# Two-layer hybrid block on one core: the second layer's first products in another order, and queries and keys copied out of PSUM ahead of their norms

## The chip, the cores and the metric

One core of one Trainium2 chip runs the whole program. The metric is the device time of one execution, in microseconds (us). Names used: PE is TensorE, DVE is VectorE, ACT is ScalarE, POOL is GpSimd, SP is the engine that issues the DMAs.

## What is computed

Two trunk layers over 512 latent tokens and 256 context tokens, 1024 features wide, in fp32:

```python
for l in range(2):
    h  = modulate(rms_norm(x,  g_mix[l]), sh1,  sc1)      # latents
    hc = modulate(rms_norm(xc, g_mix[l]), csh1, csc1)     # context
    aq, ak, av, bu, bv, cin, dq, dk, dv = split_cols(h @ w_in[l])
    # the last layer takes only the keys and values of A and D from the context
    out_a = window_attention(rope(rms_norm(aq)), rope(rms_norm(ak)), av, ...)
    out_b = spatial_gating(bu, bv, ...)
    out_c = multiscale_pool(cin, ...)
    out_d = neighbourhood_attention(rms_norm(dq), rms_norm(dk), dv, ...)
    x = x + g1 * (concat(out_a, out_b, out_c, out_d) @ w_out[l])
    x = x + g2 * swiglu(modulate(rms_norm(x, g_ffn[l]), sh2, sc2))
    # and the same for xc, in the first layer only
```

## The kernel before

**Numbers.** Every large product is made of three matmuls (`mm3`, lines 65 to 67): each operand is split into a high and a low fp32r half, and high x high, high x low and low x high are summed in PSUM. Weights come by DMA into `raw` (3 buffers) and are split by ACT (line 82) and DVE or POOL (line 83) into `w` (6 buffers) or `mraw`.

**Layout.** The stream is kept feature-major: eight tiles `x` of 128 features x 768 tokens, latents in columns 0 to 511, context in 512 to 767. The norm over features is a matmul with ones over the sum of squares (`norm_scale`, line 290), a reciprocal root by ten small DVE steps (`rsqrt`, lines 100 to 109), and a matmul that spreads the root over the partitions (`norm_spread`, line 299), which ACT copies to a `row` tile, called `r` (line 301).

**First products.** Three column groups of the input projection, C (two halves) and the values of D (two halves), don't wait for the norm: `scaled` multiplies `x` by its gain only, and the root is multiplied in when the result is taken out of PSUM. Their PSUM banks are `pj` x2 (first half of C), `sc` x2 (second half of C), `po` and `pt` (first half of D's values), and `tq` and `md` (second half of D's values), so all eight banks are full when they end. `c_take` empties the `pj` and `sc` banks (line 784), `d_values` the others (lines 586 to 596).

**Normed input.** The other groups take `h`, eight tiles made by `normed` (lines 304 to 316): for latents and then for context of each of the eight k, gain and root (DVE line 313, or ACT line 310 and POOL line 311 for the k in a list), shift (ACT line 314) and low half (DVE line 315).

**Queries and keys.** `tok_proj` makes two token tiles of 256 columns in one bank (`pj` or `sc`, 48 matmuls). `post_qk` then squares them from PSUM on ACT (line 479), sums (DVE line 481), takes the root (`rsqrt`), multiplies by it from PSUM (DVE line 484), then gain, rotary, transposes into `tq` (PE line 510) and splits into the tiles that attention reads (lines 525, 526 and 531 to 533). The tiles of `post` have 4 buffers. In the second layer the order in the program is `d_ctx` (keys of D from the context), `d_proj(0)`, the attention of D's first pair, `d_proj(1)`, and so on to A and B.

**Order.** Each engine works through its own queue in order. The queues are written at build time by a scheduler that takes program order as priority and places instructions by its own estimate of when they can start; `issue_after(ins)` puts an instruction behind another one on its engine.

Of the kernel before, what the change touches and what calls it, by code (L numbers as in the profile page):

```python
# [39 lines left out]
def hybrid_block(ctx: ExitStack, tc, t, out):  # L40
# [9 lines left out]
    def tile(tag, shape, dtype=F32):  # L50
        return sb.tile(shape, dtype, tag=tag, name=tag, bufs=BUFS[tag])
# [217 lines left out]
    class Squares:  # L269
# [5 lines left out]
        def add(self, x, eng=V):  # L275
# [6 lines left out]
            S.activation(sq[:, :n], x[:, :n], AF.Square)  # L282
            eng.tensor_add(self.acc[:, :n], self.acc[:, :n], sq[:, :n])

    def norm_scale(sq, segs):

        n = segs[-1][1] // 128
        ps = psum("tq")
        for i in range(n):
            T.matmul(ps[:, i:i + 1], sq.acc[:, 128 * i:128 * i + 128], ones[:, 0:1], start=True, stop=True)  # L290
        return rsqrt(ps[:, :n], n, 1.0 / D, EPS)

    def norm_spread(r, segs, tags):

        out = tile("row", [128, NT])
        for (s0, s1, v), tag in zip(segs, tags):
            bc = psum(tag)
            for i in range(s0 // 128, s1 // 128):
                T.matmul(bc[:, 128 * i - s0:128 * i - s0 + 128], r[:, i:i + 1].to_broadcast([128, 128]), ident,
                         start=True, stop=True)  # L300
            S.activation(out[:, s0:s1], bc[:, :s1 - s0], AF.Copy)
        return out

    def normed(x, r, gain, sh, eng):

        h = tile("h", [128, 2, NT], F32R)
        for s0, s1, v in segs_all:
            u, hi, lo = x[:, s0:s1], h[:, 0, s0:s1], h[:, 1, s0:s1]
            if eng is G:
                S.activation(u, u, AF.Copy, scale=gain[:, v:v + 1])  # L310
                G.tensor_mul(u, u, r[:, s0:s1])
            else:
                V.scalar_tensor_tensor(u, u, gain[:, v:v + 1], r[:, s0:s1], op0=OP.mult, op1=OP.mult)
            S.activation(hi, u, AF.Identity, bias=sh[:, v:v + 1])
            V.scalar_tensor_tensor(lo, u, sh[:, v:v + 1], hi.bitcast(F32), op0=OP.add, op1=OP.subtract)
        return h

    def per_feature(m, u, k):
        return m[:, u, k // 4, k % 4]
# [65 lines left out]
    for l in range(DEPTH):  # L385
# [13 lines left out]
        if l == 0:  # L399
            xs, hu, ready = [None] * KT, [None] * KT, set()  # L400
            sq = Squares(segs_all)
            ws = [[], [], []]
            for what, k in START.split():
                k = int(k)
                if what == "w":
                    for w, (name, g) in zip(ws, first):
                        w += wsplit(t[name][0, g][:, 512 * k:512 * k + 512])
                    continue
                if what == "s":
                    mod_slab(k, mods[0], bg)  # L410
                else:
                    xs[k] = load_x(t["xt"][:, k])
                    sq.add(xs[k], G if k in (1, 3, 4, 5, 6, 7) else V)
                if k in ready:
                    hu[k] = scaled(xs[k], a[:, 0, k], shift(k), segs_all)
                ready.add(k)
                if what + str(k) == "s4":
                    rr = norm_scale(sq, segs_all)
                if what + str(k) == "s5":
                    r = norm_spread(rr, segs_all, ("md", "md"))  # L420
            first = ws
            mods.append(new_mod(1))
        else:
            r = norm_spread(norm_scale(sq, segs_all), segs_all, ("tq", "tq"))
            first = [feat_units(*x) for x in first]
        fcuts = [cuts_lat if last else cuts_all] * 2 + [cuts_all]
        pss = [[psum(x) for x in y] for y in (("pj", "pj"), ("sc", "sc"), ("po", "pt"))]
        for k in range(KT):
            for w, ct, ps in zip(first, fcuts, pss):
                scaled_proj(w, hu[k], ct, ps, k)  # L430
        pss.append([psum(x) for x in ("tq", "md")])
        w = feat_units("win_dv", 1, "mraw")
        for k in range(KT):
            scaled_proj(w, hu[k], cuts_all, pss[3], k)
        h = []
        for k in range(KT):
            with behind([3, -1, 7, 7, 7, 7, 7, 7][k] if l == 0 else -1):
                h.append(normed(xs[k], r, a[:, 0, k], shift(k), G if k in [[0, 1, 3, 6], [0, 3, 6]][l] else V))


        if l == 0:
# [31 lines left out]
        def post_qk(ps, b, nq, nk, gain, ng, rope, Q, K, window, c0=0):  # L473

            nh = nq + nk
            p3 = ps.rearrange("p (i x) -> p i x", i=2)[:, :, c0:c0 + 64 * nh].rearrange("p i (h d) -> p i h d", d=64)
            flat = "p i h d -> p (i h) d"
            s2 = tile("post", [128, 2, nh, 64])
            S.activation(s2, p3, AF.Square)
            ss = small.tile([128, 8], F32, tag="ss", name="ss")  # L480
            V.tensor_reduce(ss[:, :2 * nh], s2.rearrange(flat), axis=AX.X, op=OP.add)
            r = rsqrt(ss[:, :2 * nh], 2 * nh, 1.0 / 64, EPS).rearrange("p (i h) -> p i h", i=2)
            n_ = tile("post", [128, 2, nh, 64])
            V.tensor_tensor(n_, p3, r.unsqueeze(3).to_broadcast([128, 2, nh, 64]), op=OP.mult)
            if ng:
                V.tensor_tensor(n_[:, :, 0:ng], n_[:, :, 0:ng],
                                gain.unsqueeze(1).unsqueeze(1).to_broadcast([128, 2, ng, 64]), op=OP.mult)
            if rope:
                rot = tile("post", [128, 2, nh, 64])
                for i in range(2):  # L490
                    nv = n_[:, i].rearrange("p h (x f c) -> p h x f c", x=2, f=2)
                    rv = rot[:, i].rearrange("p h (x f c) -> p h x f c", x=2, f=2)
                    sv = sinT[:, b + i].rearrange("p (x f c) -> p x f c", x=2, f=2)
                    for f in range(2):
                        V.tensor_tensor(rv[:, :, :, f], nv[:, :, :, 1 - f],
                                        sv[:, :, f].unsqueeze(1).to_broadcast([128, nh, 2, 16]), op=OP.mult)
                V.tensor_tensor(n_, n_, cosT[:, b:b + 2].unsqueeze(2).to_broadcast([128, 2, nh, 64]), op=OP.mult)
                V.tensor_add(n_, n_, rot)
            t0 = 128 * b

            w = window and b < 4
            pt = psum("tq")
            for j in range(nh // 2):
                for i in range(2):
                    dst = pt[:, 256 * j:256 * j + 256]
                    if w and 2 * j < nq:
                        dst = dst.rearrange("p (w i r c) -> p i r w c", w=4, i=2, r=2)[:, i]
                    else:
                        dst = dst[:, 128 * i:128 * i + 128]
                    T.transpose(dst, n_[:, i, 2 * j:2 * j + 2], ident)  # L510
            halves = [slice(64 * e, 64 * e + 64) for e in range(2)]
            for j in range(nh // 2):
                src = pt[:, 256 * j:256 * j + 256]
                if 2 * j < nq:

                    for e in range(2):
                        own, other = [Q[j][halves[x], e] for x in (e, 1 - e)]
                        if w:
                            own, other = [x[:, :SEQ].rearrange("p (w y x) -> p w y x", w=4, y=2)[:, :, b // 2]
                                          for x in (own, other)]  # L520
                            y = src[halves[e]].rearrange("p (w x) -> p w x", w=4)
                        else:
                            own, other = [x[:, t0:t0 + 256] for x in (own, other)]
                            y = src[halves[e]]
                        S.activation(own, y, AF.Copy)
                        V.tensor_sub(other, y, own.bitcast(F32))
                else:

                    for e in range(2):
                        own, other = [K[0][halves[x], e, t0:t0 + 256] for x in (e, 1 - e)]  # L530
                        S.activation(own, src[halves[e]], AF.Copy)
                        S.activation(other, src[halves[e]], AF.Copy)
                        V.tensor_sub(K[1][halves[e], e, t0:t0 + 256], src[halves[e]], own.bitcast(F32))
# [312 lines left out]
                             nsink[:, p:p + 3:2], mix[p])  # L846

        if last:
            csh = [c_take(c, pss[c]) for c in range(2)]
            v0 = d_values(pss[2], "row")  # L850
            v1 = d_values(pss[3], "mraw")
            kc = d_ctx()
            q0 = d_proj(0, kc[0])
# [9 lines left out]
            a_group(1, *ga)  # L863
            b_fin(*gb)
        else:
            csh = [c_take(c, pss[c]) for c in range(2)]
            v0 = d_values(pss[2], "row")
            v1 = d_values(pss[3], "mraw")
# [227 lines left out]
```

## Time and profile before

| | us |
|---|---|
| median of three runs | 1555.96 |
| the three runs | 1555.71 to 1559.7 |
| the profiled execution | 1556.92 |
| its span, first to last instruction | 1555.1 |
| PE busy in the span | 1514.8 |
| DVE busy in the span | 957.6 |
| ACT busy in the span | 620.8 |

All times below are us from the start of the span of the profiled execution. The second layer begins at about 930; its input projection and attention last until about 1147, and the output projection and the feed-forward part follow.

### The profile page before, as it was taken

How to read it: one execution, taken by the hardware profiler on the slowest of the kernel's cores; microseconds unless marked ns; L12 is line 12 of the kernel's file. 1: busy time of each engine (PE TensorE's matmuls, PEld its weight loads, DVE VectorE, ACT ScalarE, POOL GpSimd, SP SyncE). 2: the span in 40 equal slices, each digit the busy share in tenths (PEclk: the TensorE clock that was granted, in tenths of full speed). 3: DMA queues.
4: the chain of work that ended last, by engine and by line, in shares of the span. 5: the costliest groups of instructions: out<-in, count | busy, mean ns of one | idle time of the engine just before them, and what ended most of it. 6: DMA issues, size and time to landing. Idle time of an engine off the chain costs nothing.

```text
span 1555.1 us, 26167 instructions
## 1 busy us (share of the span) xinstructions
PE 1514.8 (97%) x10098; PEld 1332.3 (86%) x10098; DVE 957.6 (62%) x2317; ACT 620.8 (40%) x1278; POOL 113.6 (7%) x107
## 2 busy tenths in 40 slices
PE   7899999999999999999999998899999999999999
PEld 4688787788888888888888887888889998998997
DVE  4689877686486624843384467789956553454553
ACT  5547655643322112221222354467754332332331
POOL 2321200100000000000000004432000000000000
PEclk9899999999999999999999999999999999999999
DMA  8343223342243313622272231211233233323223
GB/s 311 119 149 100 87 87 108 124 140 74 88 143 123 109 65 112 223 60 68 90 243 65 75 114 55 80 34 44 64 102 101 95 91 99 94 85 103 95 84 100
DMA packets 79324, 163.39 MB, mean 105 GB/s; under 512 B 12000, under 2 KB 17760, under 8 KB 79200
## 3 DMA queue, kind: packets, MB, share of 16 engines
q1 hardware_dynamic: 79200, 161.73, 32.7%
q8 instruction: 79, 1.29, 0.3%
q14 instruction: 45, 0.37, 0.1%
HBM read 157.50 MB, written 4.19 MB: 104 GB/s over the span
## 4 chain that ended last, share of the span: by engine, by line
PE 88%; DVE 6%; DMA 3%; ACT 1%; issue 1%; SPq 0%; POOL 0%; ACTq 0%; POOLq 0%
PE pj L65 9%; PE pj L66 9%; PE pj L67 9%; PE sc L65 6%; PE sc L66 6%; PE sc L67 6%; PE tq L65 3%; PE tq L66 3%; PE po L66 3%; PE po L65 3%; PE tq L67 3%; PE po L67 3%; PE po L349 3%; PE pt L66 2%; PE pt L65 2%; PE pt L67 2%
## 5 line engine op out<-in xcount | busy, mean ns | idle before, releaser
L82 ACT ACTIVATE w<-raw 128x512 fp32r<-128x512 f32 x368 | 227.8, 622 | 627.0 <-PE sc L67 157.0
L83 DVE TENSOR_TENSOR w<-raw,w 128x512 fp32r<-128x512 f32 x336 | 226.2, 676 | 241.2 <-ACT w L82 240.5
L65 PE MATMUL pj<-w,h 128*128 128x256 f32 x480 | 139.6, 291 | 13.2 <-DVE x L784 7.7
L66 PE MATMUL pj<-w,h 128*128 128x256 f32 x480 | 139.2, 290 | 0.0
L67 PE MATMUL pj<-w,h 128*128 128x256 f32 x480 | 138.8, 290 | 0.0
L66 PE MATMUL pj<-st,w 128*128 128x258 f32 (+2 forms) x384 | 120.0, 313 | 3.0 <-DVE st L254 3.0
L65 PE MATMUL pj<-st,w 128*128 128x258 f32 (+2 forms) x384 | 120.2, 314 | 1.4 <-ACT st L253 1.2
L66 PE MATMUL sc<-st,w 128*128 128x258 f32 (+2 forms) x384 | 119.3, 311 | 0.0
L67 PE MATMUL pj<-st,w 128*128 128x258 f32 (+2 forms) x384 | 119.3, 311 | 0.0
L65 PE MATMUL sc<-st,w 128*128 128x258 f32 (+2 forms) x384 | 119.2, 311 | 0.0
L67 PE MATMUL sc<-st,w 128*128 128x258 f32 (+2 forms) x384 | 118.8, 310 | 0.0
L65 PEld LDWEIGHTS pj<-w,h 128*128 128x128 f32 x480 | 93.3, 194 | 20.4 <-issue 10.4
L83 POOL TENSOR_TENSOR w<-raw,w 128x512 fp32r<-128x512 f32 x32 | 42.6, 1342 | 747.5 <-ACT w L82 723.0
L66 PEld LDWEIGHTS pj<-w,h 128*128 128x128 f32 x480 | 93.4, 195 | 1.8 <-issue 0.9
L67 PEld LDWEIGHTS pj<-w,h 128*128 128x128 f32 x480 | 93.2, 194 | 0.4 <-issue 0.3
L65 PEld LDWEIGHTS pj<-st,w 128*128 128x128 f32 x384 | 73.0, 190 | 8.4 <-ACT st L253 2.4
L66 PEld LDWEIGHTS pj<-st,w 128*128 128x128 f32 x384 | 72.7, 189 | 7.8 <-DVE st L254 3.2
L67 PEld LDWEIGHTS pj<-st,w 128*128 128x128 f32 x384 | 72.6, 189 | 5.5 <-issue 1.7
L65 PEld LDWEIGHTS sc<-st,w 128*128 128x128 f32 x384 | 72.8, 190 | 4.5
L66 PEld LDWEIGHTS sc<-st,w 128*128 128x128 f32 x384 | 72.4, 188 | 4.2
L67 PEld LDWEIGHTS sc<-st,w 128*128 128x128 f32 x384 | 72.3, 189 | 4.0
L65 PE MATMUL po<-st,w 128*128 128x512 f32 (+1 forms) x192 | 66.1, 344 | 0.0
(308 smaller groups left out, 4122.1 us busy)
## 6 DMA issues: line engine op xcount, KB each, us to landing
mraw<-in_wmod SPq DMA_DIRECT2D x80, 512.0 KB, 3.7
raw<-in_wg SPq DMA_DIRECT2D x88, 256.0 KB, 2.6
raw<-in_wu SPq DMA_DIRECT2D x88, 256.0 KB, 2.6
raw<-in_wd SPq DMA_DIRECT2D x64, 256.0 KB, 2.7
h<-in_wslab SPq DMA_DIRECT2D x16, 512.0 KB, 7.9
raw<-in_wout SPq DMA_DIRECT2D x32, 256.0 KB, 2.6
x<-in_xt SPq DMA_DIRECT2D x16, 384.0 KB, 5.7
raw<-in_wd SPq DMA_DIRECT2D x32, 192.0 KB, 2.4
```

What stands on the lines that cost most here:

```text
L65: T.matmul(ps, ah, bh, start=start, stop=False)
L66: T.matmul(ps, ah, bl, start=False, stop=False)
L67: T.matmul(ps, al, bh, start=False, stop=stop)
L82: S.activation(w[:, 0, :n], raw, AF.Copy)
L83: eng.tensor_sub(w[:, 1, :n], raw, w[:, 0, :n].bitcast(F32))
L349: T.matmul(o[64 * hh:64 * hh + 64, :128], vs[hh][lo:hi], pts[i, hh], start=i == 0, stop=i == n - 1)
```

## The change

Four edits. In the second layer the first products run group by group (all eight k of one group) in place of k by k, with the norm's matmuls placed by `issue_after`: the ones-matmuls are issued before unit 6 (of 24 units, eight k for each of three groups) and the spreading ones before unit 10. `norm_spread` spreads the context segment before the latent one, everywhere it is used, and in the second layer into two banks (`tq` and `md`) in place of one. `normed` works on one segment at a time: the context of all eight k first; the latents follow later in program order, in the second layer the first two k ahead of `c_take` and the rest behind the first `d_values`. POOL's list of k in the second layer becomes 2, 4, 6 in place of 0, 3, 6. In `post_qk`, in both layers, ACT copies the queries and keys from PSUM to a `post` tile, ahead of the squares, and DVE multiplies the copy by the root in place.

```diff
     def norm_spread(r, segs, tags):
...
-        for (s0, s1, v), tag in zip(segs, tags):
+        for (s0, s1, v), tag in reversed(list(zip(segs, tags))):
...
-    def normed(x, r, gain, sh, eng):
-
-        h = tile("h", [128, 2, NT], F32R)
-        for s0, s1, v in segs_all:
-            u, hi, lo = x[:, s0:s1], h[:, 0, s0:s1], h[:, 1, s0:s1]
+    def normed(h, x, r, gain, sh, eng, seg):
+
+        s0, s1, v = seg
+        u, hi, lo = x[:, s0:s1], h[:, 0, s0:s1], h[:, 1, s0:s1]
...
-            r = norm_spread(norm_scale(sq, segs_all), segs_all, ("tq", "tq"))
+            r = norm_spread(norm_scale(sq, segs_all), segs_all, ("tq", "md"))
...
-        for k in range(KT):
-            for w, ct, ps in zip(first, fcuts, pss):
-                scaled_proj(w, hu[k], ct, ps, k)
+        if last:
+
+            for j, (w, ct, ps) in enumerate(zip(first, fcuts, pss)):
+                for k in range(KT):
+                    with ExitStack() as st:
+                        for mark, n in (("scale", 6), ("spread", 10)):
+                            if 8 * j + k >= n:
+                                st.enter_context(tc.issue_after(marks[mark].ins))
+                        scaled_proj(w, hu[k], ct, ps, k)
+        else:
+            for k in range(KT):
+                for w, ct, ps in zip(first, fcuts, pss):
+                    scaled_proj(w, hu[k], ct, ps, k)
...
-                h.append(normed(xs[k], r, a[:, 0, k], shift(k), G if k in [[0, 1, 3, 6], [0, 3, 6]][l] else V))
+        h = [tile("h", [128, 2, NT], F32R) for _ in range(KT)]
+
+        def normalise(seg, k0=0, k1=KT):
+            for k in range(k0, k1):
+                with behind([3, -1, 7, 7, 7, 7, 7, 7][k] if l == 0 else -1):
+                    normed(h[k], xs[k], r, a[:, 0, k], shift(k), G if k in [[0, 1, 3, 6], [2, 4, 6]][l] else V, seg)
+
+        normalise(segs_all[1])
...
+            n_ = tile("post", [128, 2, nh, 64])
+            S.activation(n_, p3, AF.Copy)
             s2 = tile("post", [128, 2, nh, 64])
             S.activation(s2, p3, AF.Square)
...
-            n_ = tile("post", [128, 2, nh, 64])
-            V.tensor_tensor(n_, p3, r.unsqueeze(3).to_broadcast([128, 2, nh, 64]), op=OP.mult)
+            V.tensor_tensor(n_, n_, r.unsqueeze(3).to_broadcast([128, 2, nh, 64]), op=OP.mult)
...
         if last:
+
+            normalise(segs_all[0], 0, 2)
             csh = [c_take(c, pss[c]) for c in range(2)]
             v0 = d_values(pss[2], "row")
+            normalise(segs_all[0], 2)
             v1 = d_values(pss[3], "mraw")
...
         else:
+            normalise(segs_all[0])
             csh = [c_take(c, pss[c]) for c in range(2)]
```

## Rows read from the trace of the kernel before

**Rows 1.** Page, busy time of each engine.

```profile
PE 1514.8 (97%) x10098; PEld 1332.3 (86%) x10098; DVE 957.6 (62%) x2317; ACT 620.8 (40%) x1278; POOL 113.6 (7%) x107
```

**Rows 2.** Waits of PE, 930 to 1150: total, times, longest.

```profile
PE pj L65 <- DVE x L784: 7.2, 1, 7.2
PE pj L65 <- ACT st L532: 4.9, 1, 4.9
```

**Rows 3.** Busy time by stage: window, length, engines, granted PE clock, DMA.

```profile
60.00:340.00 280.00, 275.77 (x2077) 231.76 (x2077) 224.96 (x669) 163.11 (x382) 36.51 (x37) 0.99 0.34 111
961.50:1050.00 88.50, 73.64 (x572) 69.64 (x574) 72.55 (x223) 46.37 (x107) 34.70 (x34) 0.92 0.16 53
1050.00:1110.00 60.00, 60.00 (x514) 53.93 (x511) 56.15 (x192) 42.38 (x104) 8.76 (x7) 1.00 0.14 46
1110.00:1147.00 37.00, 37.00 (x263) 29.37 (x263) 23.84 (x71) 23.03 (x52) 0.00 (x0) 1.00 0.32 101
```

**Rows 4.** Timeline of PE, second layer's first products: start, duration.

```profile
930.12 0.28 PE L65 MATMUL pj<-st,w 128*128 128x256 f32 x1
...
936.77 1.40 PE L290 MATMUL tq<-ones,row 128*128 128x1 f32 x12
...
943.34 1.05 PE L299 MATMUL tq<-ident,ry 128*128 128x128 f32 x8
...
947.68 0.60 PE L299 MATMUL tq<-ident,ry 128*128 128x128 f32 x4
...
961.07 0.28 PE L67 MATMUL md<-st,mraw 128*128 128x258 f32 x1
```

**Rows 5.** Timeline of DVE over the same stretch.

```profile
933.27 0.95 DVE L283 TENSOR_TENSOR row<-row 128x768 f32<-128x768 f32 x1
...
938.20 0.17 DVE L100 TENSOR_SCALAR rx<-tq 128x6 f32<-128x6 f32 x1 [3.58 <-PE tq L290]
...
945.07 6.61 DVE L313 SCALAR_TENSOR_TENSOR x<-x,a,row 128x512 f32<-128x512 f32 x5 [4.88 <-ACT row L301]
...
959.10 3.44 DVE L313 SCALAR_TENSOR_TENSOR x<-x,a,row 128x256 f32<-128x256 f32 x5
...
964.86 3.24 DVE L315 SCALAR_TENSOR_TENSOR h<-x,mod,h 128x256 fp32r<-128x256 f32 x8
...
970.21 0.41 DVE L586 TENSOR_TENSOR mraw<-md,row 128x256 f32<-128x256 f32 x1
```

**Rows 6.** Timeline of ACT: the roots' copies, and a square of queries and keys.

```profile
944.43 0.60 ACT L301 ACTIVATE row<-tq 128x512 f32<-128x512 f32 x1 [2.10 <-PE tq L299]
...
951.67 0.36 ACT L301 ACTIVATE row<-tq 128x256 f32<-128x256 f32 x1
...
998.64 0.60 ACT L479 ACTIVATE post<-pj 128x512 f32<-128x512 f32 x1
```

**Rows 7.** Chain that ended last, 936 to 1060: PE after its two waits.

```profile
968.58 0.55 PE pj L65
...
971.48 0.15 PE pj L65
971.99 0.12 PE pj L66
...
1006.64 0.55 PE pj L65
...
1012.10 0.21 PE pj L65
```

**Rows 8.** Timeline of DVE ahead of the second wait.

```profile
990.99 3.42 DVE L100 TENSOR_SCALAR rx<-ss 128x8 f32<-128x8 f32 x1
...
1005.80 0.69 DVE L484 TENSOR_TENSOR post<-pj,ry 128x512 f32<-128x512 f32 x1
```

**Rows 9.** Single line: duration min/median/max in ns, first and last start.

```profile
L484 DVE TENSOR_TENSOR post<-pj,ry x21: 406/691/693, 92.0 to 1076.8; 128x512 f32<-128x512 f32 x13, 128x256 f32<-128x256 f32 x8
```

**Rows 10.** Single line: the gain after it, from SBUF; columns as before.

```profile
L486 DVE TENSOR_TENSOR post<-post,d_q_gain x10: 406/422/1382, 93.5 to 1012.2; 128x256 f32<-128x256 f32 x10
```

More of the change, by code (lines that the diff above doesn't have):

```diff
@@ L283, in add @@
             eng.tensor_add(self.acc[:, :n], self.acc[:, :n], sq[:, :n])
+    marks = {}
     def norm_scale(sq, segs):
@@ L289, in norm_scale @@
         for i in range(n):
-            T.matmul(ps[:, i:i + 1], sq.acc[:, 128 * i:128 * i + 128], ones[:, 0:1], start=True, stop=True)
+            marks["scale"] = T.matmul(ps[:, i:i + 1], sq.acc[:, 128 * i:128 * i + 128], ones[:, 0:1],
+                                      start=True, stop=True)
         return rsqrt(ps[:, :n], n, 1.0 / D, EPS)
@@ L295, in norm_spread @@
         out = tile("row", [128, NT])
-        for (s0, s1, v), tag in zip(segs, tags):
+        for (s0, s1, v), tag in reversed(list(zip(segs, tags))):
             bc = psum(tag)
             for i in range(s0 // 128, s1 // 128):
-                T.matmul(bc[:, 128 * i - s0:128 * i - s0 + 128], r[:, i:i + 1].to_broadcast([128, 128]), ident,
-                         start=True, stop=True)
+                marks["spread"] = T.matmul(bc[:, 128 * i - s0:128 * i - s0 + 128],
+                                           r[:, i:i + 1].to_broadcast([128, 128]), ident, start=True, stop=True)
             S.activation(out[:, s0:s1], bc[:, :s1 - s0], AF.Copy)
         return out
-    def normed(x, r, gain, sh, eng):
-        h = tile("h", [128, 2, NT], F32R)
-        for s0, s1, v in segs_all:
-            u, hi, lo = x[:, s0:s1], h[:, 0, s0:s1], h[:, 1, s0:s1]
[L309 to L316, printed above, removed]
+    def normed(h, x, r, gain, sh, eng, seg):
+        s0, s1, v = seg
+        u, hi, lo = x[:, s0:s1], h[:, 0, s0:s1], h[:, 1, s0:s1]
+        if eng is G:
+            S.activation(u, u, AF.Copy, scale=gain[:, v:v + 1])
+            G.tensor_mul(u, u, r[:, s0:s1])
+        else:
+            V.scalar_tensor_tensor(u, u, gain[:, v:v + 1], r[:, s0:s1], op0=OP.mult, op1=OP.mult)
+        S.activation(hi, u, AF.Identity, bias=sh[:, v:v + 1])
+        V.scalar_tensor_tensor(lo, u, sh[:, v:v + 1], hi.bitcast(F32), op0=OP.add, op1=OP.subtract)
     def per_feature(m, u, k):
@@ L427, in hybrid_block @@
         pss = [[psum(x) for x in y] for y in (("pj", "pj"), ("sc", "sc"), ("po", "pt"))]
-        for k in range(KT):
-            for w, ct, ps in zip(first, fcuts, pss):
-                scaled_proj(w, hu[k], ct, ps, k)
+        if last:
[6 more added lines that the diff above has]
+                        scaled_proj(w, hu[k], ct, ps, k)
+        else:
+            for k in range(KT):
+                for w, ct, ps in zip(first, fcuts, pss):
+                    scaled_proj(w, hu[k], ct, ps, k)
         pss.append([psum(x) for x in ("tq", "md")])
@@ L434, in hybrid_block @@
             scaled_proj(w, hu[k], cuts_all, pss[3], k)
-        h = []
-        for k in range(KT):
-            with behind([3, -1, 7, 7, 7, 7, 7, 7][k] if l == 0 else -1):
-                h.append(normed(xs[k], r, a[:, 0, k], shift(k), G if k in [[0, 1, 3, 6], [0, 3, 6]][l] else V))
+        h = [tile("h", [128, 2, NT], F32R) for _ in range(KT)]
[4 more added lines that the diff above has]
+        normalise(segs_all[1])
         if l == 0:
```

## The prediction

> **What bounds the kernel now.** I read the page's busy times first: PE works 1514.8 of the span's 1555.1 us, and DVE 957.6 [rows 1]. So PE sets the time, its work is not changed, and the change can only win what PE loses between its matmuls, or lose by adding to it. Next the waits of PE in the second layer's projection and attention: one of 7.2 us on `c_take` (line 784) and one of 4.9 us that is put down to line 532 [rows 2]. The table by stage says what that is of the whole: from 961.5 to 1050 PE is busy 73.6 of 88.5 us, so 14.9 are lost, the two waits and 2.8 us of small ones; from 1050 to 1147 nothing is lost [rows 3]. The reader is to see there also that DVE is busy 56.2 of the 60 us from 1050 on: it is a second engine close to its limit, right behind the place where the gain would be.
>
> **Why PE waits at 961.** The last first product ends at 961.35 [rows 4], and PE starts on the context's keys at 968.58 [rows 7]. Those need a `pj` bank and the context part of all eight `h`. The timeline of DVE shows a block without a gap from 945.07 to 970.62: latents' line 313, their line 315, the context's line 313 only at 959.10, its line 315 last of all at 964.86, and `c_take` behind that [rows 5]. The block starts at 945.07 because `r` is late: the squares' sum is done at 934.22 [rows 5], the ones-matmuls start at 936.77, the spreading at 943.34, and the context's spreading at 947.68 [rows 4], as it waits for the one bank that ACT is copying from. ACT's copies end at 945.03 and 952.03 [rows 6].
>
> **The head of the layer, after.** I put the new order on the clock of the old one. First products start at 930.12 [rows 4]; a matmul of 256 columns takes 0.12 [rows 7], so a unit of six takes 0.72, and the six units ahead of the ones-matmuls end at 934.4, when the sum (934.22) is there. The ones-matmuls take 1.40 [rows 4]: 935.8. The root is ten DVE steps of 0.17 [rows 5], with gaps some 2.0: 937.8. Four units cover it, to 938.7. Spreading took 1.05 + 0.60 [rows 4]; the context's third of it comes first, then its copy of 0.36 [rows 6]: context `r` at about 939.6, latent `r` (0.60 to copy) at about 941. That is 12 and 4 us earlier. DVE's block was 25.55 us long [rows 5] with nothing idle; started at 939.6 it ends at 965.1. In it the context comes first: five of 0.69 (3.44 / 5) and eight of 0.41 (3.24 / 8), 6.7 us, to 946.3; two k of latents, four operations of 1.32 (6.61 / 5), to 951.6; `c_take`, four operations of 256 columns at the 0.41 of line 586 and two tiny ones, 1.8, to 953.4. PE needs both at 961.35, 8 us later. The work that hides the block is the rest of the first products; without it (were `r` late as before) the wait would be back whole. What is late next is the latents' `h`: PE has 48 matmuls of the context, 5.8 us, to 967.1, and the block ends at 965.1. Two us of slack, so I cost it at nothing. The weights pass no queue that gets longer: the first group's two `w` buffers come free after eight units in place of half-way through all, and the steps moved issue no DMA; the constants' DMAs on SP wait for none of them.
>
> The wait costs more than 7.2. After it PE's matmuls stand 0.21 apart, half speed, until 971.48: 12 in 2.90 us where 12 x 0.12 = 1.44 would do [rows 7]. The mean granted clock from 961.5 to 1050 is 0.92 [rows 3]. So the head is worth 7.2 + 1.5 = **8.7 us**, and I take it whole; its lower bound is 0 (below).
>
> **The copy ahead of the norms.** The second wait, 4.9 us long [rows 2], ends at 1006.64 [rows 7], just when line 484 (1005.80 + 0.69) has read the bank [rows 8]: the row names line 532, the bank is what is waited for. Line 484 is late because the root ahead of it sat behind a DVE step of 3.42 us [rows 8], 0.17 elsewhere [rows 5]. With the copy the bank is free when ACT has read it twice. Here ACT squared at 998.64 in 0.60 [rows 6]; with the copy before it the bank is free at 999.9, ahead of the 1001.7 at which PE comes to it. The bank wait goes, and with it the half-speed stretch behind it, 24 matmuls in 5.46 us where 2.88 would do: 4.9 + 2.6 = 7.5 us at most. What can be late next: a tile of `post` is now held from the copy to the transposes, and there are four; and DVE has the same chain to do. Between 0 and 7.5 I take **5.0**, nearer to the upper end since the row shows the bank free in time, and less than all since DVE's 3.42 is not touched. The small waits, 2.8 us, hang on the same chains of DVE in attention: between 0 and 2.8, taken **0.8**.
>
> What it adds: 23 copies on ACT, 0.36 to 0.60 each, some 12 us over two layers. ACT is busy 42 of 60 us at its fullest here [rows 3], so they fit; each also stands ahead of its square, in the latency of its chain. In the first layer PE is busy 275.8 of 280 us from 60 on [rows 3]: the other reorderings there can win 4.2 at most, and the 12 copies of that layer can lose up to 7 if all were on the path. I take 0.
>
> DVE's multiplication changes from a PSUM source to an SBUF one. From PSUM line 484 never took over 0.69 [rows 9]. Line 486, with its operands in SBUF, takes 0.42 as a rule and 1.38 at worst [rows 10]; laid beside POOL's timeline, its long ones are those under a POOL instruction. The second layer has eleven of line 484, nine of them before 1050, where POOL is busy 34.7 of 88.5 us [rows 3]: some three would lie under POOL, so 0 to 3 x 0.96 = 2.9 us of DVE. I take **1.0** lost, as not each lands on the path. The Trainium skill (SBUF — State Buffer, "SBUF: two separate sides") has a rule that speaks against this edit: a DVE operation with two SBUF inputs and a GpSimd one that reads SBUF take one port pair by turns, and the loser waits out the whole instruction. By that rule the copy buys its bank with all 2.9 us, if DVE sets the end; the trace agrees as far as the 1.38 goes.
>
> **Sum.** 8.7 + 5.0 + 0.8 - 1.0 = 13.5 us off. The profiled execution took 1556.92, 1.8 more than its span, and would take 1543.4; the median of the runs is 0.96 below it, so 1542.5.
>
> **Rivals.**
> *All of it goes.* 8.7 + 7.5 + 2.8 = 19.0, and some of the first layer's 4.2. For it: from 1110 to 1147 DVE is busy only 23.8 of 37 us [rows 3], so it can take work earlier. Time 1535 to 1537.
> *DVE takes over.* The head is won, but DVE is busy 94% from 1050 to 1110 [rows 3], the matmuls that fill PE there run out sooner, and the second and the small waits come back on softmax or on `post`. Against it: DVE also starts 5 us earlier and no longer stands idle between 970.6 and the first squares of the context's keys. 8.7 less 1.0 to 2.9: time 1547 to 1550, or 1552 if half the head returns as well.
> *The change does not do what it says.* The queues are fixed from an estimate. If DVE's queue has `d_values` of the third group, or POOL's k, before their inputs are there, the block waits for PE at 952 and the latents' `h` is late by as much as was won. Time 1553 to 1557.
> *Slower: the copies hold ACT.* A copy that finds no free `post` tile stops ACT's whole queue, with the exponentials and the weight splits behind it, until an earlier chain's transposes are done. The only price of such a chain here is PE's wait of 4.9 [rows 2]: five of the 23 at 4.9 cost 24.5 against 13.5 won, 1567. It decides from 18.2 us on, 0.8 for each copy. Against it: three chains fit the four tiles unless rotary takes a third.
>
> **How the numbers follow.** Forecast 0.42 (its own range 1538 to 1547), all of it 0.15, DVE takes over 0.25, not as said 0.08, slower 0.10. Faster, by over 0.3% (4.7 us, about what a measurement of this kernel can tell from no change), is the first three: 0.82; same 0.08; slower 0.10. The range from 1535 to 1553 leaves out the slower case and most of the fourth.
>
> **What would show it.** The ones-matmuls at about 934.4 and spreading by 940, context first. DVE's block starting near 939.6, with line 784 ahead of most of the latents. No wait of PE on line 784, and PE running from the last first product into line 65 of the context's keys at full clock. No wait at the third projection after `d_proj(0)`; in its place perhaps ACT waiting for a `post` tile. Line 484 with a maximum over 1 us. I am wrong if PE's idle time between 930 and 1150 stays over 10 us, or if the first layer's PE idle time grows by more than 3 us.

## The result and the profile after

The changed kernel takes 1547.82 us, median of four runs (1547.29 to 1549.23), and the kernel before took 1555.84 beside it (1555.3 to 1559.7): a ratio of 0.9943, with a 95% interval of 0.9931 to 0.9956. By the medians that is 8.0 us faster, where 13.5 were forecast; the time lies in the whole range of 1535 to 1553, and above the forecast's own 1538 to 1547. The profiled execution took 1548.02 us, with a span of 1546.2: 8.9 us less, in both, than the execution that the sum was made against.

Engine totals of the page for the kernel after, against [rows 1]: PE issues the same matmuls, ACT has the 23 copies more.

```profile
PE 1510.5 (98%) x10098; PEld 1329.1 (86%) x10098; DVE 961.0 (62%) x2317; ACT 628.9 (41%) x1301; POOL 117.5 (8%) x107
```

Waits of PE from 930 to 1150 in the kernel after (total, times, longest), against [rows 2]. Its line numbers lie 16 higher in attention than before: `c_take` is line 800, the multiplication 500.

```profile
PE tq L526 <- DVE st L549: 2.7, 1, 2.7
PE po L350 <- ACT pts L345: 1.5, 2, 0.7
PE sc L368 <- DVE T L646: 1.4, 3, 0.7
PE tq L611 <- ACT row L603: 1.1, 1, 1.1
PE sc L369 <- DVE st L549: 0.8, 1, 0.8
PE pj L65 <- DVE st L758: 0.5, 1, 0.5
PE pj L65 <- DVE x L800: 0.2, 1, 0.2
```

Both large waits are gone. In their place stand one of 2.7 us for the bank of the transposes and a row of small ones, 8.2 us in all, where the kernel before has 15.0. So the prediction's first sign of being wrong, over 10 us, did not come.

Busy time by stage, the kernel after, columns as in [rows 3] (the last window is shorter here, since attention ends at 1138.5, where it ended at 1148.0; from 1110 to 1140 the kernel before loses nothing either):

```profile
60.00:340.00 280.00, 274.71 (x2079) 230.48 (x2078) 226.88 (x671) 165.28 (x390) 40.27 (x36) 1.00 0.35 112
961.50:1050.00 88.50, 83.18 (x675) 78.23 (x674) 77.37 (x247) 57.23 (x137) 36.49 (x36) 0.98 0.16 51
1050.00:1110.00 60.00, 58.45 (x471) 50.72 (x471) 55.37 (x173) 41.55 (x99) 6.12 (x5) 1.00 0.26 82
1110.00:1140.00 30.00, 28.51 (x215) 22.79 (x214) 14.96 (x49) 16.90 (x38) 0.00 (x0) 1.00 0.15 48
```

From 961.5 to 1050 PE loses 5.3 us where it lost 14.9, and the granted clock is 0.98 where it was 0.92. From 1050 on it loses 3.0 us where it lost nothing. So part of the gain is given back there. In the first layer's stretch, 60 to 340, it loses 5.3 us where it lost 4.2: the second sign of being wrong, 3 us more, did not come either.

The timeline of PE, the kernel after, against [rows 4] and the start of [rows 7]:

```profile
933.42 1.39 PE L292 MATMUL tq<-ones,row 128*128 128x1 f32 x12
...
937.62 0.60 PE L302 MATMUL md<-ident,ry 128*128 128x128 f32 x4
...
938.06 1.06 PE L302 MATMUL tq<-ident,ry 128*128 128x128 f32 x8
...
960.50 0.36 PE L65 MATMUL pj<-w,h 128*128 128x256 f32 x1 [0.19 <-DVE x L800]
...
1002.96 1.11 PE L526 MATMUL tq<-ident,post 128*128 128x128 f32 x4 [2.70 <-DVE st L549]
```

The timeline of DVE, the kernel after, against [rows 5]:

```profile
938.68 11.09 DVE L315 SCALAR_TENSOR_TENSOR x<-x,a,row 128x256 f32<-128x256 f32 x10 [1.85 <-ACT row L304]
...
949.68 10.34 DVE L317 SCALAR_TENSOR_TENSOR h<-x,mod,h 128x256 fp32r<-128x256 f32 x14
...
959.94 0.74 DVE L800 TENSOR_TENSOR x<-pj,row 128x256 f32<-128x256 f32 x2
...
964.52 0.41 DVE L602 TENSOR_TENSOR mraw<-md,row 128x256 f32<-128x256 f32 x1
```

The head runs nearly as said. The whole layer starts 1.0 us earlier, and with it the ones-matmuls (933.42 for 934.4) and the block of DVE (938.68 for 939.6); the spreading is done by 939.1, and the context's keys stand behind a wait of only 0.19. But `c_take` is not "ahead of most of the latents". It starts at 959.94, where 951.6 was expected, and PE takes it up at once: the 8 us of slack did not exist. In this queue all ten of DVE's scalings (line 315) and 14 of the 16 low halves (line 317) stand ahead of it.

Where the span went is read from four points of PE's timeline: the second layer's first product, the first product of the context's keys, the first product of the output projection's fifth tile (of eight, into `sc`), PE's last. The first half of the output projection does not follow attention but is mixed with it: its first product stands at 1111.24 before and at 1092.75 after. The third point is where attention and that half are done; the expectations below call it the output projection. Stretches between the points, in us:

```
                 2nd layer   to keys   to fifth     to the
                 starts                tile         end
before           930.12      38.46     186.99       395.78
after            929.13      31.37     185.62       396.33
```

1.0 came from the first layer, 7.1 from the head, 1.4 from all of attention and the first half of the output projection behind it, and 0.5 was lost at the end: 8.9. Each is a single execution, and others of the same first layer differ by more than a microsecond, as is shown below.

### The profile page after: what moved, and what is told of

Read it like the earlier page. It is cut to its first block, busy times and chain, and to the rows that moved or that the text cites. A ratio compares the mean times of both kernels' runs of the same rounds, so it can differ in the third digit from the quotient of the medians.

```text
span 1546.2 us, 26176 instructions
## 1 busy us (share of the span) xinstructions
PE 1510.5 (98%) x10098; PEld 1329.1 (86%) x10098; DVE 961.0 (62%) x2317; ACT 628.9 (41%) x1301; POOL 117.5 (8%) x107
## 4 chain that ended last, share of the span: by engine, by line
PE 84%; DVE 9%; DMA 3%; issue 2%; ACT 1%; POOL 1%; SPq 0%; ACTq 0%; POOLq 0%
PE pj L65 8%; PE pj L66 8%; PE pj L67 8%; PE sc L66 6%; PE sc L65 6%; PE sc L67 6%; PE tq L65 3%; PE tq L66 3%; PE tq L67 3%; PE po L65 3%; PE po L66 3%; PE po L67 3%; PE po L350 2%; PE pt L66 2%; PE pt L65 2%; PE pt L67 2%
## 5 line engine op out<-in xcount | busy, mean ns | idle before, releaser
L65 PEld LDWEIGHTS pj<-w,h 128*128 128x128 f32 x480 | 91.8, 192 | 6.1 <-ACT st L548 0.8
L67 PEld LDWEIGHTS pj<-w,h 128*128 128x128 f32 x480 | 92.1, 192 | 2.6 <-issue 2.5
L66 PEld LDWEIGHTS pj<-w,h 128*128 128x128 f32 x480 | 92.2, 192 | 1.6 <-DVE st L542 0.8
## 6 DMA issues: line engine op xcount, KB each, us to landing
raw<-in_wd SPq DMA_DIRECT2D x32, 192.0 KB, 2.3
```

The costliest lines, as they stand in the source:

```text
L65: T.matmul(ps, ah, bh, start=start, stop=False)
L66: T.matmul(ps, ah, bl, start=False, stop=False)
L67: T.matmul(ps, al, bh, start=False, stop=stop)
```

## Experiments

The theory at the outset was that the order wins the head and the copy wins the second wait, but that DVE hands part of it back. The main rival was that the copy wins nothing. Each run has the kernel before beside it on its chip; ratios are to that, with 95% intervals.

**The parts alone.** `order_only` is the kernel after without the copy; `copy_only` is the kernel before with it.

```diff
 order_only, against the kernel after
-            n_ = tile("post", [128, 2, nh, 64])
-            S.activation(n_, p3, AF.Copy)
...
-            V.tensor_tensor(n_, n_, r.unsqueeze(3)...
+            n_ = tile("post", [128, 2, nh, 64])
+            V.tensor_tensor(n_, p3, r.unsqueeze(3)...
 copy_only, against the kernel before: the same lines the other way round
```

> The reordering of norm and first products in both layers, with the keys and queries multiplied from PSUM as before. Theory (the head and the copy win in turn, DVE gives part back): the 7.2 us wait on c_take is gone, the bank wait near 1001 is back at 3 to 6 us with the half-speed stretch behind it; about 1550 to 1552. Rival (all of the gain is the head's, the copy is worth nothing): 1547 to 1548.5, the same as the changed kernel.

> The copy ahead of the norms alone, all orders as before. Theory: the 7.2 us wait on c_take stays, the bank wait of 4.9 us goes and a smaller wait on the transposes' bank takes its place; gain 2 to 5 us, 1551 to 1554. Rival (without the head DVE is no further than before and the copy only lengthens chains): within 1.5 us of 1555.8 or slower.

Measured: `order_only` 1545.37 us, 0.9931 (0.9919 to 0.9944), below both times expected; `copy_only` 1555.28, 0.9992 (0.9983 to 1.0), as the rival said. The order alone is all of the gain. Waits of PE, 930 to 1150, `order_only`:

```profile
PE pj L65 <- DVE post L499: 5.3, 1, 5.3
...
PE tq L610 <- ACT row L602: 1.1, 1, 1.1
```

and `copy_only`:

```profile
PE pj L65 <- DVE x L785: 7.2, 1, 7.2
PE sc L367 <- DVE T L631: 4.6, 6, 1.4
PE tq L511 <- DVE st L534: 3.1, 2, 2.4
```

The kernel before has, beside [rows 2], for the last two of these lines:

```profile
PE sc L367 <- DVE T L630: 0.7, 1, 0.7
PE tq L510 <- DVE st L533: 0.6, 1, 0.6
```

Without the copy the bank wait is there, 5.3 us, and named by its multiplication. With the copy alone it is gone; the waits for line 631 (a step of the softmax) grow from 0.7 to 4.6 and for the transposes' bank from 0.6 to 3.1. The copy does what it says, and PE waits a little later instead, most of it for DVE: all waits from 930 to 1150 come to 15.2 us with the copy alone against 15.0 before, and to 8.2 in the kernel after against 8.1 in `order_only`.

The four points of PE's timeline, as above, for the parts and for the repeats that follow below:

```
                 2nd layer   to keys   to fifth     to the
                 starts                tile         end
copy_only        931.22      38.47     184.96       396.32
order_only       928.71      31.44     183.34       395.78
order_again      928.50      31.50     184.02       395.78
after_again      928.62      31.50     185.86       396.32
```

In the old order the copy makes the stretch behind the keys 2.0 us shorter, and the time comes out nearly the same, since in these executions the second layer starts 1.1 later and the end takes 0.5 more. In the new order that stretch is 1.6 to 2.5 us longer with the copy, and the end again 0.5.

The stages of `order_only` say the same of the new order, from 1050 on, against the two last windows of the kernel after:

```profile
961.00:1050.00 89.00, 81.32 (x664) 76.55 (x663) 77.04 (x255) 54.98 (x134) 35.34 (x34) 0.96 0.16 50
1050.00:1110.00 60.00, 59.84 (x506) 54.21 (x503) 55.47 (x172) 41.34 (x97) 8.29 (x6) 1.00 0.21 68
1110.00:1143.00 33.00, 32.88 (x217) 26.81 (x216) 16.93 (x48) 17.18 (x40) 0.00 (x0) 1.00 0.30 89
```

It loses 7.7 us up to 1050, 2.4 more than the kernel after, and 0.3 in the 93 us behind, where the kernel after loses 3.0 in 90.

**The reversed spreading alone**, the kernel before with the one line of `norm_spread`.

```diff
-        for (s0, s1, v), tag in zip(segs, tags):
+        for (s0, s1, v), tag in reversed(list(zip(segs, tags))):
```

> The context segment's root spread first, nothing else. Theory (the first layer's gain of 1 us comes from a shorter idle time of PE at 48 to 55 and less half speed after it): 0.5 to 2 us faster, with a granted clock from 0 to 60 of over 0.95 where it was 0.92. Rival (the first layer's start is set by its DMAs whatever is spread first): within 0.5 us of 1555.8 and the clock as before.

Measured: 1553.91 us, 0.9981 (0.9971 to 0.9991), 1.4 to 4.5 us where 0.5 to 2 were expected, with runs from 1551.0 to 1556.2; the profiled one is the longest of them. Its waits of PE, 930 to 1150:

```profile
PE pj L65 <- DVE post L484: 5.6, 2, 4.9
...
PE pj L65 <- DVE x L784: 1.8, 1, 1.8
```

The wait on `c_take` falls from 7.2 to 1.8, and the gain in time is still only a third of the change's: in the profiled run the stretch from the keys to the fifth tile takes 192.0 us, 5.0 more than before, and the bank wait stays. The timeline of DVE:

```profile
944.15 3.61 DVE L313 SCALAR_TENSOR_TENSOR x<-x,a,row 128x256 f32<-128x256 f32 x5 [4.22 <-ACT row L301]
...
962.47 0.74 DVE L784 TENSOR_TENSOR x<-pj,row 128x256 f32<-128x256 f32 x2
...
964.33 4.97 DVE L315 SCALAR_TENSOR_TENSOR h<-x,mod,h 128x512 fp32r<-128x512 f32 x9
```

The block starts 0.9 us earlier than before [rows 5]; the wait is short because this queue has `c_take` ahead of nine low halves.

**A second bank for the transposes**, the kernel after; it goes for the 2.7.

```diff
-            pt = psum("tq")
+            pt = psum("po" if last and qk[0] % 2 and qk[0] < 6 else "tq")
```

> The changed kernel, with the transposes of the first six groups of queries and keys of the second layer going in turn to the banks tq and po in place of tq alone. Theory (the 2.7 us wait near 1000 is the one bank that DVE empties late): that wait goes or falls under 1 us, with 1 to 1.8 us of half speed behind it; 1544 to 1546. Rival (DVE sets the pace, the wait only moves to the next step that needs DVE): 1547 to 1548.5, PE's idle time between 990 and 1060 the same within 1 us.

Measured: 1552.56 us, 0.9977 (0.9969 to 0.9986), slower than the kernel after by 4.7 and than both times expected. The wait of 2.7 is gone and others for `sc`, 3.2 and 2.4 us, stand in its place: here too a freed bank alone is worth nothing. The edit also lends the transposes a bank that attention's outputs use, so it does not tell what a bank of their own would do. The run shows a place where the copy made the multiplication slow (line 502 here), in the timelines of DVE

```profile
982.53 1.81 DVE L502 TENSOR_TENSOR post<-post,ry 128x512 f32<-128x512 f32 x1
```

and of POOL:

```profile
982.51 3.00 POOL L83 TENSOR_TENSOR w<-raw,w 128x512 fp32r<-128x512 f32 x2 [0.75 <-ACT w L82]
```

**The change again, and two copies only.** `after_again` is the kernel after; `copy_two` copies only in the two chains (the fifth and sixth of the second layer) ahead of the old bank wait.

```diff
+            early = last and qk[0] in (4, 5)
...
+            if early:
                 n_ = tile("post", [128, 2, nh, 64])
                 S.activation(n_, p3, AF.Copy)
```

> The changed kernel once more, beside the others on one chip. Theory (the copy is worth nothing as the whole stands): 1546.5 to 1548.5, within 1 us of or above the kernel with the orders alone, which took 0.9931 of the kernel before. Rival (the copy helps, the chips differ): clearly below 0.9931.

> The orders of the changed kernel, with the copy made for two groups alone, the two of the second pair of D's heads in the second layer, whose banks PE waits for; all others multiply from PSUM. Theory (the copy frees the bank that matters, and what ate its gain was the latency and DVE's port in the other 21): the 5.3 us wait goes, 1542 to 1544. Rival (DVE sets the pace behind that bank, so the wait moves to the transposes or the softmax whichever way the bank is freed): 1545 to 1548.

Measured: 1547.85 us, 0.9949 (0.9937 to 0.9962), and 1547.18, 0.9945 (0.9931 to 0.9958). In `copy_two` a bank wait of 3.1 us stays, put down to the square (line 501 there), which reads the bank right behind the copy (line 499). Its timeline of ACT says why:

```profile
996.22 0.38 ACT L554 ACTIVATE st<-tq 64x256 fp32r<-64x256 f32 x1 [3.35 <-DVE st L549]
...
997.01 0.60 ACT L499 ACTIVATE post<-pj 128x512 f32<-128x512 f32 x1
```

The copy and the square stand in ACT's queue behind an operation that waited 3.35 us for DVE. Moving a bank's release from DVE to ACT does not take DVE out of it when ACT's next instruction waits for DVE.

**Less work under POOL.** `no_pool` is the kernel after, `order_no_pool` is `order_only`; in both POOL's subtraction for low halves of the second layer's weights of A and D is left out and ACT writes a plain copy in its place.

```diff
-            eng.tensor_sub(w[:, 1, :n], raw, w[:, 0, :n].bitcast(F32))
+            S.activation(w[:, 1, :n], raw, AF.Copy)      (A and D, second layer)
```

> The changed kernel with the low halves of the second layer's weights of A and D written by a copy on ACT, in place of POOL's subtraction; it leaves out that subtraction, so these low halves are wrong. Theory (DVE is slowed by sharing with POOL, and that is what eats the copy's gain): DVE's busy time from 938 to 1050 falls by 4 to 10 us, its small steps never over 0.3, the 2.7 us wait goes, 1542 to 1545. Rival (DVE's own work sets the pace, or ACT with 14 more copies): 1546.5 to 1549.

> The orders alone, with the second layer's low halves of A and D written by ACT in place of POOL's subtraction (which leaves that subtraction out, as in the earlier run). With the copy that kernel took 1543.9, 0.9922, 182.1 us from the context's keys to the output projection in the profile. Theory (with POOL out of the way DVE has room, and the freed bank is worth something): without the copy 1 to 4 us slower than with it, 1545 to 1548. Rival (the copy is worth nothing with DVE relieved either): 1541 to 1544.5.

Measured: 1543.94 us, 0.9922 (0.991 to 0.9935), and 1542.65, 0.9913 (0.9899 to 0.9926). Busy time from 961.5 to 1050 in `no_pool`:

```profile
961.50:1050.00 88.50, 85.76 (x715) 81.47 (x715) 66.75 (x241) 63.78 (x152) 20.97 (x21) 1.00 0.20 62
```

DVE is busy 66.8 us there, not 77.4, with nearly the same instructions. Over the whole span its 2317 instructions take 943.3 us, and 961.0 in the kernel after: the operations are the same, and without POOL's subtractions beside them they are 17.7 us shorter. By the medians that is worth 3.9 us with the copy and 2.7 without it (there the intervals overlap). And with DVE relieved the copy still gains nothing: 1543.94 against 1542.65, with intervals that overlap.

**The orders taken apart.** `k_by_k` is `order_only` with the first products in the old order, k by k, and without the marks that hold them behind the ones-matmuls and the spreading.

```diff
-            for j, (w, ct, ps) in enumerate(zip(first, fcuts, pss)):
-                for k in range(KT):
-                    ... issue_after(marks[mark].ins) ...
+            for k in range(KT):
+                for w, ct, ps in zip(first, fcuts, pss):
+                    scaled_proj(w, hu[k], ct, ps, k)
```

> The orders alone without the group by group order and its marks: the first products of the second layer k by k as before, context ahead of latents, context's root spread first into its own bank, no copy. Theory (what the head needs is the early root, which only the marks give): c_take comes 3 to 6 us late again, a wait of PE of 2 to 5 us at 961, 1548 to 1551. Rival (context first is enough, since the context's part was what came last): no wait over 1 us at 961, 1544 to 1546.5.

Measured: 1553.79 us, 0.9987 (0.9978 to 0.9996). Waits of PE, 930 to 1150:

```profile
PE pj L65 <- DVE x L789: 5.1, 1, 5.1
...
```

and DVE's block:

```profile
945.02 10.03 DVE L315 SCALAR_TENSOR_TENSOR x<-x,a,row 128x256 f32<-128x256 f32 x10 [4.22 <-ACT row L304]
...
966.53 0.74 DVE L789 TENSOR_TENSOR x<-pj,row 128x256 f32<-128x256 f32 x2
```

The time is above both that were expected. The block starts 6.3 us later than in the kernel after, where it started before, and `c_take` stands at its end. The early `r` comes from the group order and its marks together; without them 0.13% is left of the 0.69% that `order_only` gains.

**Against the copy's latency.** `square_first` is the kernel after with the square ahead of the copy, so that the chain to the root is as short as before; `order_again` is `order_only`.

```diff
-            n_ = tile("post", [128, 2, nh, 64])
-            S.activation(n_, p3, AF.Copy)
             s2 = tile("post", [128, 2, nh, 64])
             S.activation(s2, p3, AF.Square)
+            n_ = tile("post", [128, 2, nh, 64])
+            S.activation(n_, p3, AF.Copy)
```

> The changed kernel with ACT's square ahead of its copy, so that the chain of the norm starts as early as without the copy and the bank comes free as early as with it. Theory A (the copy costs by standing ahead of the square in every chain): 1 to 3 us below the changed kernel, 1544.5 to 1546.5. Theory B (DVE sets the pace behind it, whichever is first): 1547 to 1548.5, within 1 us of the changed kernel.

> The orders alone once more, as the one to compare the other three with. Theory (the copy costs 2 us in the new order): 0.992 to 0.994 of the kernel before. Rival (the two are the same and the first run was lucky): 0.9945 to 0.9955.

Measured: 1551.85 us, 0.9971 (0.9961 to 0.9981), and 1545.36, 0.993 (0.9917 to 0.9942). That the copy costs by its place ahead of the square finds no support: behind it the kernel is slower by 4.0, above both times expected. But the run is no clean test. Its second layer starts 2.6 us later than in the kernel after, at 931.73, and three of its multiplications started under operations of POOL, and took 1.68, 1.62 and 1.01 us; the longest is the maximum in its single line:

```profile
L500 DVE TENSOR_TENSOR post<-post,ry x23: 406/691/1678, 89.7 to 1065.1; 128x512 f32<-128x512 f32 x15, 128x256 f32<-128x256 f32 x8
```

`order_again` repeats 1545.37 to a hundredth, so the orders without the copy stand at 0.993 and the full change at 0.9943 and 0.9949. Each pair of intervals overlaps, but the nine runs with the copy take 1546.8 to 1549.3 and the eleven without it 1543.3 to 1548.0, where the medians of the kernel before beside them lie within 0.8 of each other.

**No gain on POOL in the head.** `order_no_g` is `order_only` with POOL's three k of the second layer given to DVE.

```diff
-  G if k in [[0, 1, 3, 6], [2, 4, 6]][l] else V
+  G if k in [[0, 1, 3, 6], []][l] else V
```

> The orders alone, with no k of the second layer's norm on POOL: DVE does all eight. Theory (the block of DVE at the head is long because DVE and POOL take turns, 1.1 us for operations that take 0.42 and 0.75 alone): the block is 1 to 4 us shorter although it has six operations more, c_take is earlier, 0.5 to 2 us faster than the orders alone. Rival (POOL's share is a net relief): the block is longer, PE waits 1 to 3 us on c_take, 1 to 3 us slower.

Measured: 1543.19 us, 0.9917 (0.9904 to 0.9931), 2.2 less than `order_only`, whose interval overlaps, and 4.6 less than the kernel after: by the medians the fastest kernel here that computes everything. Its timeline of DVE has `c_take` at

```profile
957.31 0.74 DVE L799 TENSOR_TENSOR x<-pj,row 128x256 f32<-128x256 f32 x2
```

3.4 us ahead of PE, and the waits of 0.2 on it and of 1.1 behind it are gone. The groups of DVE's scalings from 938 to 965, by size (count, busy time, mean ns), in the kernel after

```profile
L315 DVE SCALAR_TENSOR_TENSOR x<-x,a,row 128x256 f32<-128x256 f32 x5 | 5.7, 1197 | 1.9 <-ACT row L304 1.9
L315 DVE SCALAR_TENSOR_TENSOR x<-x,a,row 128x512 f32<-128x512 f32 x5 | 5.5, 1159 | 0.0
```

and in `order_no_g`:

```profile
L315 DVE SCALAR_TENSOR_TENSOR x<-x,a,row 128x512 f32<-128x512 f32 x8 | 5.5, 740 | 0.0
L315 DVE SCALAR_TENSOR_TENSOR x<-x,a,row 128x256 f32<-128x256 f32 x8 | 3.3, 478 | 1.9 <-ACT row L304 1.9
```

DVE does 16 of these steps in 8.8 us, where it did 10 in 11.2 with POOL's share beside it. POOL is not idle meanwhile: the second layer's weight splits that it still has wait instead, as its timeline shows:

```profile
942.50 14.97 POOL L83 TENSOR_TENSOR w<-raw,w 128x512 fp32r<-128x512 f32 x1 [3.52 <-ACT w L82]
```

One such instruction takes 1.28 us as a rule. Here it ends at 957.47, no more than that behind the last of DVE's low halves (956.32), where DVE has come to the operations that read PSUM.

## Why the prediction was right, and where it was not

**What bounds the kernel** held. DVE's and ACT's totals rose by 3 and 8 us while the kernel became faster; but for the first layer's 1.0, what it won lies between the second layer's start and the output projection's fifth tile, where PE lost time.

**The head, 8.7 us: mechanism right, size nearly.** The stretch from the first product to the keys is 7.1 us shorter: the wait of 7.2 fell to 0.2. The half speed behind it went too (the granted clock is 1.00 from 961 to 973), but the keys now lead into a new wait of 1.1 on the transposes of `d_values` (line 611). The steps went at the predicted times, DVE's block lasted 26.2 us (938.68 to 964.93) where 25.6 were put down, and `k_by_k` shows that the early `r` is what does it. The wrong step is "to 951.6" and "to 953.4", the place of `c_take` in DVE's queue and with it "8 us later". I read the block's order from the order of the calls; the planner set three scalings and four low halves of the latents more ahead of it. The prices of the steps were not at fault in sum: at the prediction's own (0.69 and 1.32 for the scalings, 0.41 and 1.26 for the low halves, 7.58 / 6 in [rows 5]) the 24 steps ahead of `c_take` come to 20.9 us, and they took 21.3. So the slack was nothing, and `c_take` came 0.2 us late; that it was not more is luck. `order_no_g` takes POOL's share of the block away and has 3.4 us of slack.

**The copy, 5.0 of 0 to 7.5: this is the step that failed.** "The bank wait goes, and with it the half-speed stretch" is so, in the waits after and in `copy_only`. That most of it would stay won is not: alone the copy gives 0.0 to 0.17%, at most 2.6 us, and on top of the new order nothing: by the medians a loss of 2.5 (1547.8 against 1545.4, twice), below the lower bound of 0. The bank was one of several things that wait for DVE at that place: with it free, PE came sooner to the transposes' bank, to softmax, to `sc`. The prediction had seen DVE at 94% from 1050 on and had named this as a rival; it is the case that came true, in its time (1547 to 1550), in its waits, and in that PE's filling matmuls ran out sooner: the output projection, next in line, begins at 1092.75 where it began at 1111.24. In part that is luck: the rival took 1.0 to 2.9 us off the head for multiplications beside POOL, which did not come, and the copy's loss, which it did not have, is about as large. The range held since it took in this rival, not because the forecast's sum was right. What spoke for giving it more stands in the same table [rows 3]: already from 961.5 to 1050, where both waits of PE lay, DVE was busy 72.6 of 88.5 us. And the 3.42 us of [rows 8] belong to the root of the tile before (multiplied at 996.34); in the root of the waited-for tile itself three steps from 1000.00 on took 1.17, 1.23 and 0.98 us, also beside POOL.

Two counts in the sums are one short: the half-speed stretches hold 13 and 25 matmuls, not 12 and 24. That makes them 1.3 and 2.5 us, for 1.5 and 2.6, and changes nothing in the argument.

Why the copy costs in the new order, rather than nothing, stays open. PE's idle time does not hold it: between the keys and the fifth tile PE stands idle 8.4 us in the kernel after and 8.0 in `order_only`, for the same 1388 matmuls, while the stretch is 2.3 us longer. What can be seen is the order: with the copy PE takes up the output projection earlier (1092.75 and 1092.65, against 1102.84 and 1103.27 without it) and ends attention later (1138.5 and 1138.4, against 1133.7 and 1134.2). Another bank for the transposes did not bring the time back, nor did the square ahead of the copy, in a run that is no clean test; ACT's queue delays the copy in one variant; and with POOL's work left out a difference of 1.3 stays, within the intervals. Every edit of these lines makes the planner lay out all queues anew, and from the keys to the fifth tile variants take from 180.7 to 192.0 us; a difference of 2.5 between two of them needn't have one cause.

**Small waits, 0.8:** they grew instead. The prediction's 2.8 us are 5.3 in the listing after, the 2.7 of the transposes' bank and the 0.2 of `c_take` not counted.

**Contention of the multiplication, 1.0 of 0 to 2.9: mis-sized, nothing here.** Single line of DVE in the kernel after, against [rows 9]:

```profile
L500 DVE TENSOR_TENSOR post<-post,ry x23: 417/691/694, 91.1 to 1065.5; 128x512 f32<-128x512 f32 x15, 128x256 f32<-128x256 f32 x8
```

The maximum of 0.694 is the same from SBUF as from PSUM: none of the second layer's eleven came to lie beside a POOL operation. The "maximum over 1 us" that was to show the step right didn't come. Where one did start under an operation of POOL, it took 1.81 us in `two_tq` and, three times, 1.01 to 1.68 in `square_first`. From PSUM no such price shows: in the kernel before, the multiplication at 1005.80 took its 0.69 [rows 8] beside POOL's weight split from 1005.24 to 1006.50. The Trainium skill (SBUF — State Buffer, "SBUF: two separate sides") says of a DVE operation with two SBUF inputs and a GpSimd one that reads SBUF that the one that starts second is blocked until the other ends. The trace of `two_tq` agrees nearly: POOL started at 982.51, DVE at 982.53, and 1.81 is the 0.69 of the work and 1.12 more, less than the 1.28 of POOL's first instruction. In `copy_only` DVE started first, at 989.10 against 989.17: there the multiplication kept its 0.69, and POOL's instruction took 1.77. So the price, 0.96 each in the prediction, was about right, and in the kernel after its occasion was missing.

**First layer, 0:** it gained 1.0. Busy time from 52 to 64, the kernel before,

```profile
52.00:64.00 12.00, 10.78 (x55) 6.70 (x56) 9.46 (x20) 9.12 (x21) 8.13 (x9) 0.52 0.25 79
```

and `spread_only`:

```profile
52.00:64.00 12.00, 9.38 (x53) 7.11 (x54) 11.33 (x18) 9.09 (x20) 8.56 (x11) 0.86 0.27 89
```

The granted clock there is 0.86 and not 0.52 (0.86 in the kernel after too). It is not the same in all: the twelve profiles here with the reversed spreading have 0.60 to 1.00 in that stretch, `copy_only` without it 0.54. The first token projection starts 2.1 us earlier in `spread_only` (74.11 against 76.17), 2.4 in the kernel after (73.74), and at 72.56 to 74.11 in all twelve, against 75.18 in `copy_only`; that speaks for the reversed spreading, which serves both layers. But more than half of it is lost again by the second layer's start, and the twelve start it anywhere from 928.50 to 931.73, the other two at 930.12 and 931.22. So the 1.0 is not more than what such executions differ by, and what the twelve copies of the first layer cost can't be told from them: with the reversed spreading the second layer starts at 928.50 to 930.75 without the copies and at 928.62 to 931.73 with them.

**Slower, 0.10:** ACT's wait for a `post` tile ahead of a square (line 496) came to 1.3 us from 930 to 1150, once, and no wait of PE in the listing names the copy.

## What to carry to other kernels

A wait that an engine close to its limit ends need not be worth its length: price the removal by the next thing that waits for the same engine (here that engine was 82% busy in the stretch, and removing a wait of 4.9 us was worth nothing that the times show). A reorder that starts an engine's block earlier moves everything behind it and can be counted; moving a release from one in-order queue to another only counts where that queue doesn't itself wait for the first. And run the parts alone: here the order without the copy, with POOL's share of the head given back to DVE, takes 1543.19 us where the whole change takes 1547.82 (0.9917 and 0.9943 of the kernel before, intervals that just meet).

## What the runs showed of the hardware that was not expected

What POOL cost DVE was larger than the work it took over. The scaling with gain and root, 256 columns from SBUF, took 1.20 us beside POOL's steps and 0.48 where DVE had all eight k and POOL was idle up to 942.50; with six of these steps more, two for each k, its block was shorter. It works the other way too: an instruction of POOL that takes 1.28 us as a rule took 14.97 beside the rest of that block. The price falls on the smallest steps too: in the kernel after, DVE's steps of the root, 8 columns here, 0.17 us with 6 columns in [rows 5], stand beside POOL's subtraction as

```profile
993.97 1.22 DVE L103 SCALAR_TENSOR_TENSOR rz<-rz,rx 128x8 f32<-128x8 f32 x1
...
995.22 1.22 DVE L104 SCALAR_TENSOR_TENSOR ry<-rz,ry 128x8 f32<-128x8 f32 x1
```

with POOL's own row over the same time:

```profile
993.87 2.56 POOL L83 TENSOR_TENSOR w<-raw,w 128x512 fp32r<-128x512 f32 x2
```

Each of these two steps ends when one of POOL's two instructions, 1.28 us, has ended. It can be more than one: the 3.42 us of [rows 8], from 990.99 to 994.41, lie beside this row of POOL in the kernel before,

```profile
990.11 3.79 POOL L83 TENSOR_TENSOR w<-raw,w 128x512 fp32r<-128x512 f32 x3
993.85 0.53 POOL L795 MEMSET st<- 128x528 f32 x1
```

and end with it.
